# Moving the split weights to other byte offsets in SBUF: one layer of a hybrid decoder on one core

## The chip, the core and the metric

The kernel runs on one core of a Trainium2 chip. The metric is the device time of one execution, in microseconds (us). Before the change it is 1136.88 us, the median of three runs (1136.14, 1136.88 and 1137.68). The profile shown here is of one further execution, which took 1139.12 us.

## What is computed

One decoder layer over 512 tokens of width 1024, all in float32: a half-step SwiGLU feed-forward block (width 2816), a combined projection that feeds a gated spatial mixer and a dilated windowed attention, an output projection, cross-attention into 256 memory rows, a second half-step feed-forward block, and a last RMSNorm. In the reference's words:

```python
def swiglu(h, w_gate, w_up, w_down):
    return (jax.nn.silu(h @ w_gate) * (h @ w_up)) @ w_down

h = rmsnorm(x, ffn1_norm[l])
x = x + 0.5 * swiglu(h, ffn1_w_gate[l], ffn1_w_up[l], ffn1_w_down[l])
h = rmsnorm(x, mix_norm[l])
z = h @ w_in[l]
...
x = x + y @ w_out[l]
h = rmsnorm(x, cross_norm[l])
m = rmsnorm(mem, mem_norm[l])
x = x + memory_cross_attention(h, m, cross_wq[l], cross_wk[l], cross_wv[l], cross_wo[l])
h = rmsnorm(x, ffn2_norm[l])
x = x + 0.5 * swiglu(h, ffn2_w_gate[l], ffn2_w_up[l], ffn2_w_down[l])
return rmsnorm(x, final_norm)
```

## The kernel before

Activations are kept transposed: width on the 128 partitions, the 512 tokens along the free dimension, so the residual stream is eight tiles x0 to x7 of 128 x 512. To keep float32 accuracy at the rate of the rounded type float32r, every operand of a large product is split into a high part (rounded, made by an ACT copy) and a low part (the rest, made by a DVE subtraction): `hH, hL` for activations and `whi, wlo` for weights. A product is then three matmuls into one PSUM bank: high by high, high by low, low by high (`mm3`, L127 to L129).

Weights stream from HBM through `load_weight` (L109 to L119). It takes a raw tile `wraw`, sends the DMA for it on SP's queue, and splits it: ACT writes `whi` (L103), DVE writes `wlo` from `wraw` and `whi` (L104). Each of the three has three buffers of 4096 bytes per partition. In the feed-forward blocks, the query, key and output projections, the 128 x 128 block of `whi` or `wlo` is the stationary operand and the activations (512 tokens, or 256 memory rows) stream past it. In the two projections `z_block` (w_in) and the value projection of the cross-attention it is the other way round: a slice of the activations is stationary and 512 columns of `whi` or `wlo` stream. For most of the last down projection the split weights are kept: they are written into 2048-byte tiles of the activation pool instead (named `wk`), and they stream 256 tokens at a time, so that each half of the tokens can be finished apart.

The order of the work is the program's own order on each engine; the framework puts in the waits. `LAG`, `WARM` and `SB` are small numbers that set how far attention stages are skewed, how many matmuls on ones run at the start while the first weights arrive, and a buffer count.

What the change is about is where the tiles lie. Pools are laid one behind the other within each partition, in the order in which they are opened, and each tile takes a multiple of 32 bytes. The small pools end at byte 6944, which is 32 beyond a multiple of 128; a pool `fill` of `FILL = 56` words (224 bytes) follows, and so `base` (the residual stream) begins at 7168, a multiple of 1024. Every tile that a large matmul reads lies behind it, in pools whose tiles are multiples of 128 bytes: `hp` (40 tiles of 2048 bytes, the activations) begins at 37376, `wp` (three raw, three high and three low tiles of 4096 bytes) at 119296, 131584 and 143872, and the pool of the stage at hand (`ffn`, `mix` or `cross`) at 156160. All of these are multiples of 128, so before the change every operand of every large matmul begins at 0 beyond a multiple of 128.

```python
base = ctx.enter_context(tc.tile_pool(name="base", bufs=1))
hp = ctx.enter_context(tc.tile_pool(name="hp", bufs=40))
wp = ctx.enter_context(tc.tile_pool(name="wp", bufs=3))
```

Of the kernel before, what the change touches and what calls it, by code (L numbers as in the profile page):

```python
# [17 lines left out]
F32 = mybir.dt.float32  # L18
F32R = mybir.dt.float32r
# [5 lines left out]
P = 128  # L25
# [29 lines left out]
def body(tc, I, out):  # L55
    nc = tc.nc
    from contextlib import ExitStack
    ctx = ExitStack()
    with ctx:
# [3 lines left out]
        base = ctx.enter_context(tc.tile_pool(name="base", bufs=1))  # L63
        hp = ctx.enter_context(tc.tile_pool(name="hp", bufs=40))
        wp = ctx.enter_context(tc.tile_pool(name="wp", bufs=3))
        pacc = ctx.enter_context(tc.tile_pool(name="pacc", bufs=4, space=bass.MemoryType.PSUM))
        paux = ctx.enter_context(tc.tile_pool(name="paux", bufs=4, space=bass.MemoryType.PSUM))

# [33 lines left out]
        def split(hi, lo, src):  # L102
            ins = nc.scalar.activation(hi, src, AF.Copy)  # L103
            nc.vector.tensor_sub(lo, src, f32(hi))  # L104
            return ins
# [2 lines left out]

        def load_weight(src, shape, cuts=1):  # L109
            raw = wp.tile([P] + shape, F32, name="wraw", tag="wraw")  # L110
            hi = wp.tile([P] + shape, F32R, name="whi", tag="whi")
            lo = wp.tile([P] + shape, F32R, name="wlo", tag="wlo")
            step = shape[0] // cuts
            for c in range(cuts):
                p = slice(c * step, (c + 1) * step if c < cuts - 1 else shape[0])
                last["dma"] = nc.sync.dma_start(raw[:, p], src[:, p])
                last["hi"] = split(hi[:, p], lo[:, p], raw[:, p])
            return hi, lo
# [95 lines left out]
        def ffn(norm, gate, up, down, nxt, first=None, between=None):  # L214
            h = (norm.H, norm.L)
            with tc.tile_pool(name="ffn", bufs=2) as fp:
# [40 lines left out]
                for c in range(NCHUNK):  # L257
                    hid = ([], [])
                    for j in range(CF):
                        f = c * CF + j  # L260
                        ps = []
                        for src in (gate, up):
                            if f == 0 and src is gate and first is not None:
                                w = first()
                            else:
                                w = load_weight(src[f], [KD, P])
                            acc = acc_tile()
                            for k in range(KD):
                                mm3(acc, w, h, (slice(None), k), k, k == 0, k == KD - 1)
                            ps.append(acc)  # L270
                            if first is not None and f == 1 and R is None:
                                R = factor()
                        pending.append(ps)
                        if first is not None and f == 0:
                            continue
                        if R is None:
                            R = factor()
                        while pending:
                            evacuate(pending.pop(0), hid)
                    if c < NCHUNK - 1 or nxt is not None:  # L280
                        for d in range(KD):
                            w = [load_weight(down[c, d, :, j0:j1, :], [j1 - j0, P])
                                 for j0, j1 in halves]
                            down_tile(d, w, hid, slice(0, S), halves)
                            if c == NCHUNK - 1:
                                nxt.add(d)
                            elif between is not None:
                                between(d)
                        continue
# [5 lines left out]
                    def weights(d, keep):  # L295
                        if d in kept:
                            return kept[d], thirds
                        if not keep:
                            return [load_weight(down[c, d, :, j0:j1, :], [j1 - j0, P])
                                    for j0, j1 in halves], halves  # L300
                        kept[d] = []
                        for j0, j1 in thirds:
                            raw = wp.tile([P, j1 - j0, P], F32, name="wraw3", tag="wraw")
                            nc.sync.dma_start(raw, down[c, d, :, j0:j1, :])
                            pair = tuple(h_tile("wk")[:, :(j1 - j0) * P]
                                         .rearrange("p (j m) -> p j m", m=P) for _ in range(2))
                            split(*pair, raw)
                            kept[d].append(pair)
                        return kept[d], thirds
# [574 lines left out]
```

## Time and profile before

| what | before |
|---|---|
| median of three runs | 1136.88 us |
| the profiled execution | 1139.12 us |
| its span, first to last instruction | 1137.3 us |
| TensorE busy (PE) | 1121.1 us, 99% of the span, 5472 matmuls |
| weight loads (PEld) | 936.4 us, 82% |
| VectorE busy (DVE) | 589.2 us, 52% |
| ScalarE busy (ACT) | 422.6 us, 37% |
| GpSimd busy (POOL) | 66.2 us, 6% |
| mean granted TensorE clock | 0.993 |
| read from HBM | 107.78 MB, 97 GB/s over the span with the 2.10 MB written |

Rows of the profile name a group by the line in the kernel, the engine, the operation, and the tiles written and read (`acc<-hH,whi` is a matmul into `acc` whose moving operand is the first name and whose stationary operand is the second). PE is the row of the matmuls, PEld that of the weight loads. A matmul's time in a row runs from its start to the end that the profile models, so matmuls overlap each other in the records; how fast they follow one another is read from their start times.

### The profile page before, as it was taken

The numbers are of one execution on the slowest core, as the hardware profiler recorded it, in microseconds if no ns is written. First come the engines' busy times: TensorE is split into PE (matmuls) and PEld (weight loads), VectorE is DVE, ScalarE is ACT, GpSimd is POOL, SyncE is SP. The second block draws the span as 40 slices with busy tenths as digits, with TensorE's granted clock in tenths as the row PEclk, the third lists the DMA queues.
The fourth block names the chain that finished last, engine by engine and source line by source line (L and its number), as shares of the span: only waits on it lengthen the run. The fifth ranks groups of instructions, "written<-read, shape, count | busy, mean of one in ns | idle before, by whom it ended". The sixth has DMA issues, their size and how long they took to land. (4 is left out here: it accounts for less than half of the span.)

```text
span 1137.3 us, 13932 instructions
## 1 busy us (share of the span) xinstructions
PE 1121.1 (99%) x5472; PEld 936.4 (82%) x5472; DVE 589.2 (52%) x1023; ACT 422.6 (37%) x668; POOL 66.2 (6%) x82
## 2 busy tenths in 40 slices
PE   9999999999999999999999999999999999999996
PEld 7788888888888888877868988778888888888996
DVE  4544533444344456578797555455444334445542
ACT  6332322332233433567655344433222222233420
POOL 2000100000002000001121000120000000000011
PEclk9999999999999999999989999999999999999998
DMA  6322333222233423010135412132232333323511
GB/s 218 112 93 88 114 97 128 93 93 94 83 88 114 141 93 108 25 45 29 41 111 196 165 63 74 47 102 93 95 99 75 89 125 97 108 93 113 154 63 38
DMA packets 39698, 110.79 MB, mean 97 GB/s; under 512 B 4432, under 2 KB 9296, under 8 KB 39632
## 3 DMA queue, kind: packets, MB, share of 16 engines
q1 hardware_dynamic: 39632, 109.89, 30.1%
q8 instruction: 43, 0.70, 0.2%
q14 instruction: 23, 0.19, 0.1%
HBM read 107.78 MB, written 2.10 MB: 97 GB/s over the span
## 5 line engine op out<-in xcount | busy, mean ns | idle before, releaser
L103 ACT ACTIVATE whi<-wraw 128x1024 fp32r<-128x1024 f32 (+2 forms) x213 | 202.8, 953 | 522.0 <-PE acc L128 300.9
L104 DVE TENSOR_TENSOR wlo<-wraw,whi 128x1024 fp32r<-128x1024 f32 (+2 forms) x213 | 238.4, 1120 | 166.7 <-ACT whi L103 166.4
L127 PE MATMUL acc<-hH,whi 128*128 128x512 f32 x768 | 300.8, 392 | 0.6 <-ACT hH L202 0.6
L128 PE MATMUL acc<-hL,whi 128*128 128x512 f32 x768 | 299.3, 390 | 0.8 <-DVE hL L203 0.8
L129 PE MATMUL acc<-hH,wlo 128*128 128x512 f32 x768 | 299.3, 390 | 0.5 <-DVE wlo L104 0.5
L128 PEld LDWEIGHTS acc<-hL,whi 128*128 128x128 f32 x768 | 144.3, 188 | 31.6 <-DVE hL L203 1.5
L127 PEld LDWEIGHTS acc<-hH,whi 128*128 128x128 f32 x768 | 144.3, 188 | 31.6 <-ACT hH L202 1.0
L129 PEld LDWEIGHTS acc<-hH,wlo 128*128 128x128 f32 x768 | 144.2, 188 | 30.6 <-DVE wlo L104 1.0
L127 PE MATMUL acc<-hidH,whi 128*128 128x512 f32 (+1 forms) x308 | 115.5, 375 | 0.0
L129 PE MATMUL acc<-hidH,wlo 128*128 128x512 f32 (+1 forms) x308 | 115.3, 374 | 0.0
L128 PE MATMUL acc<-hidL,whi 128*128 128x512 f32 (+1 forms) x308 | 115.3, 374 | 0.0
L170 POOL TENSOR_TENSOR sq<-sq 128x512 f32<-128x512 f32 (+1 forms) x39 | 49.3, 1265 | 778.8 <-ACT sq L178 778.4
L247 DVE TENSOR_TENSOR u<-acc,R 128x512 f32<-128x512 f32 x44 | 30.4, 690 | 121.6 <-PE acc L129 121.6
L243 DVE TENSOR_TENSOR gp<-acc,R 128x512 f32<-128x512 f32 x44 | 30.4, 691 | 85.6 <-PE acc L129 81.7
L128 PEld LDWEIGHTS acc<-hidL,whi 128*128 128x128 f32 x308 | 58.0, 188 | 10.3
L127 PEld LDWEIGHTS acc<-hidH,whi 128*128 128x128 f32 x308 | 58.0, 188 | 10.2
L129 PEld LDWEIGHTS acc<-hidH,wlo 128*128 128x128 f32 x308 | 58.0, 188 | 10.2
L127 PE MATMUL acc<-whi,hH 128*128 128x512 f32 x160 | 62.6, 391 | 0.0
L129 PE MATMUL acc<-whi,hL 128*128 128x512 f32 x160 | 62.4, 390 | 0.0
L128 PE MATMUL acc<-wlo,hH 128*128 128x512 f32 x160 | 62.3, 389 | 0.0
L230 DVE SCALAR_TENSOR_TENSOR x<-acc,x 128x512 f32<-128x512 f32 (+1 forms) x40 | 23.3, 584 | 75.0 <-PE acc L129 75.0
L178 ACT ACTIVATE sq<-x 128x512 f32<-128x512 f32 (+1 forms) x48 | 26.0, 551 | 41.8 <-DVE x L230 39.2
(211 smaller groups left out, 1476.6 us busy)
## 6 DMA issues: line engine op xcount, KB each, us to landing
wraw<-up SPq DMA_DIRECT2D x44, 512.0 KB, 3.5
wraw<-gate SPq DMA_DIRECT2D x43, 512.0 KB, 3.4
wraw<-down SPq DMA_DIRECT2D x28, 384.0 KB, 3.1
wraw<-w_in SPq DMA_DIRECT2D x20, 512.0 KB, 3.5
wraw<-down SPq DMA_DIRECT2D x28, 320.0 KB, 2.8
wraw<-w_out SPq DMA_DIRECT2D x16, 256.0 KB, 2.6
wraw<-wv SPq DMA_DIRECT2D x8, 512.0 KB, 3.4
wraw<-wk SPq DMA_DIRECT2D x8, 512.0 KB, 4.0
```

The costliest lines, as they stand in the source:

```text
L103: ins = nc.scalar.activation(hi, src, AF.Copy)
L104: nc.vector.tensor_sub(lo, src, f32(hi))
L127: nc.tensor.matmul(ps, lhsT=aH, rhs=bH, start=start, stop=False)
L128: nc.tensor.matmul(ps, lhsT=aH, rhs=bL, start=False, stop=False)
L129: nc.tensor.matmul(ps, lhsT=aL, rhs=bH, start=False, stop=stop)
L170: nc.gpsimd.tensor_add(self.parts[0], self.parts[0], sq)
L178: nc.scalar.activation(sq, src, AF.Square)
L230: nc.vector.scalar_tensor_tensor(X[d][:, tok], acc, 0.5, X[d][:, tok], op0=ALU.mult, op1=ALU.add)
L243: nc.vector.tensor_mul(gp, ps[0], R)
L247: nc.vector.tensor_mul(u, ps[1], R)
```

## The change

`whi` and `wlo` leave `wp` and get pools of their own, `wh` and `wl`, each with three buffers as before. Three small pools with one tile each stand in between: 8 words (32 bytes) ahead of `wh`, 16 words (64 bytes) ahead of `wl`, and 104 words (416 bytes) behind it. Each pad tile is touched once by a memset of one element on DVE.

`wh` then begins at 131584 + 32 = 131616, which is 32 beyond a multiple of 128. Its three tiles are 12288 bytes, 96 times 128, and so `wl` begins at 131616 + 12288 + 64 = 143968, which is 96 beyond a multiple of 128. The last pad ends at 143968 + 12288 + 416 = 156672, a multiple of 512: the pool of the stage begins 512 bytes later than before, at 0 beyond a multiple of 128 again. The raw weights, the activations, the residual stream and the kept weights `wk` stay where they were or at that same residue. `load_weight` takes its two split tiles from the new pools; nothing else is edited.

```diff
@@ -63,6 +63,13 @@
         base = ctx.enter_context(tc.tile_pool(name="base", bufs=1))
         hp = ctx.enter_context(tc.tile_pool(name="hp", bufs=40))
         wp = ctx.enter_context(tc.tile_pool(name="wp", bufs=3))
+        wpad = ctx.enter_context(tc.tile_pool(name="wpad", bufs=1))
+        wh = ctx.enter_context(tc.tile_pool(name="wh", bufs=3))
+        wpad2 = ctx.enter_context(tc.tile_pool(name="wpad2", bufs=1))
+        wl = ctx.enter_context(tc.tile_pool(name="wl", bufs=3))
+        wpad3 = ctx.enter_context(tc.tile_pool(name="wpad3", bufs=1))
+        for pool, words, n in ((wpad, 8, "pad1"), (wpad2, 16, "pad2"), (wpad3, 104, "pad3")):
+            nc.vector.memset(pool.tile([P, words], F32, name=n)[:, 0:1], 0.0)
         pacc = ctx.enter_context(tc.tile_pool(name="pacc", bufs=4, space=bass.MemoryType.PSUM))
         paux = ctx.enter_context(tc.tile_pool(name="paux", bufs=4, space=bass.MemoryType.PSUM))
 
@@ -108,8 +115,8 @@
 
         def load_weight(src, shape, cuts=1):
             raw = wp.tile([P] + shape, F32, name="wraw", tag="wraw")
-            hi = wp.tile([P] + shape, F32R, name="whi", tag="whi")
-            lo = wp.tile([P] + shape, F32R, name="wlo", tag="wlo")
+            hi = wh.tile([P] + shape, F32R, name="whi", tag="whi")
+            lo = wl.tile([P] + shape, F32R, name="wlo", tag="wlo")
             step = shape[0] // cuts
             for c in range(cuts):
                 p = slice(c * step, (c + 1) * step if c < cuts - 1 else shape[0])
```

No instruction changes its place or its waits; the order differs only at the very start of DVE's program, by the three memsets. The first rows there before the change (the residual tile's number stands behind `x_`):

```order
L73 MEMSET pad 128x1
L78 MEMSET ones 128x128
L203 SCALAR_TENSOR_TENSOR hL<-x_84,gains,hH 128x512 [waits DMAHW1_49,DMAHW0_49,Activation_49]
L104 TENSOR_TENSOR wlo<-wraw,whi 128x512 [waits DMAHW2_49,Activation_49]
L104 TENSOR_TENSOR wlo<-wraw,whi 128x512 [waits DMAHW3_49,Activation_49]
```

and the same place after it, where line numbers are seven higher:

```order
L72 MEMSET pad_88 128x1
L72 MEMSET pad_90 128x1
L72 MEMSET pad_92 128x1
L80 MEMSET pad 128x1
L85 MEMSET ones 128x128
L210 SCALAR_TENSOR_TENSOR hL<-x_105,gains,hH 128x512 [waits DMAHW1_49,DMAHW0_49,Activation_49]
L111 TENSOR_TENSOR wlo<-wraw,whi 128x512 [waits DMAHW2_49,Activation_49]
L111 TENSOR_TENSOR wlo<-wraw,whi 128x512 [waits DMAHW3_49,Activation_49]
```

The memset of `ones`, for which the warm-up matmuls wait, now stands behind four small memsets instead of one.

## The prediction

> **What bounds the kernel now.** I read the page's busy times first. Its first part gives, for each engine, busy time, share of the span and number of instructions; the clock row gives the granted TensorE clock in 40 slices.
>
> ```profile
> PE 1121.1 (99%) x5472; PEld 936.4 (82%) x5472; DVE 589.2 (52%) x1023; ACT 422.6 (37%) x668; POOL 66.2 (6%) x82
> PEclk9999999999999999999989999999999999999998
> ```
>
> TensorE is busy 99% of the time, at full clock but for one slice and the end. Busy alone does not say whether it streams at its own pace or is kept waiting inside that 99%. So I looked next at stretches of the run (length in us, then busy time and count of each engine, granted clock, DMA share, GB/s).
>
> ```profile
> 60.00:150.00 90.00, 90.00 (x399) 74.57 (x398) 43.34 (x59) 28.25 (x39) 5.25 (x4) 1.00 0.32 101
> 450.00:600.00 150.00, 146.92 (x755) 115.50 (x754) 114.46 (x306) 90.69 (x203) 16.71 (x37) 0.98 0.17 54
> 780.00:1050.00 270.00, 270.00 (x1193) 223.71 (x1192) 120.49 (x147) 79.93 (x101) 0.00 (x0) 1.00 0.31 98
> ```
>
> In the feed-forward blocks PE has no idle time at all while DVE is busy 45% of the time (120.49 of 270): weights always arrive early. Only the attention stretch (450 to 600) has gaps, with DVE busy 114 of 150 us. So nearly all of the time is a number of matmuls multiplied by how fast they follow one another, and that is read from start times in the timeline. The first two rows are 18 matmuls apart with weights stationary, the next two 9 apart with weights moving, the last two 14 apart with 256 columns.
>
> ```profile
> 300.06 0.39 PE L127 MATMUL acc<-hH,whi 128*128 128x512 f32 x1
> ...
> 304.14 0.39 PE L127 MATMUL acc<-hH,whi 128*128 128x512 f32 x1
> ...
> 479.76 0.39 PE L127 MATMUL acc<-whi,hH 128*128 128x512 f32 x1
> ...
> 481.80 0.39 PE L127 MATMUL acc<-whi,hH 128*128 128x512 f32 x1
> ...
> 1069.73 0.28 PE L128 MATMUL acc<-hidL,wk 128*128 128x256 f32 x1
> ...
> 1071.41 0.28 PE L127 MATMUL acc<-hidH,wk 128*128 128x256 f32 x1
> ```
>
> 4.08 / 18 = 226.7 ns; 2.04 / 9 = 226.7 ns; 1.68 / 14 = 120.0 ns. The longer stretch agrees: 270 us with 1193 matmuls, two of them cut by its edges, is 270 / 1191 = 226.7 ns. Going from 256 to 512 columns costs 106.7 ns, so the columns of a 512-column matmul take 213.3 ns and **13.3 ns** are left that do not depend on the columns. These 13.3 ns are the only part of the steady pace that reading operands from another place could lower, and they are the same whichever operand moves and at all three places of the program. Blocks of a weight tile lie 512 bytes apart and activations 2048, so steps of 512 bytes between the two operands change nothing; steps of 32 occur in no large matmul before the change.
>
> **The change part by part.** It moves no instruction. It adds three memsets and moves two operands to starts that are 32 and 96 beyond a multiple of 128, both 32 beyond a multiple of 64. That it does so follows from the sizes in the diff, so a rival in which the tiles stay at 0 is out.
>
> *The matmuls on shifted weights.* They are counted from the groups by shape; the column behind the shape is the count, and each stands for three products.
>
> ```profile
> L127 PE MATMUL acc<-hH,whi 128*128 128x512 f32 x768 | 300.8, 392 | 0.6 <-ACT hH L202 0.6
> L127 PE MATMUL acc<-hidH,whi 128*128 128x512 f32 x264 | 103.1, 390 | 0.0
> L127 PE MATMUL acc<-whi,hH 128*128 128x512 f32 x160 | 62.6, 391 | 0.0
> L127 PE MATMUL acc<-hidH,wk 128*128 128x256 f32 x132 | 37.4, 284 | 0.0
> L127 PE MATMUL acc<-yH,whi 128*128 128x512 f32 x64 | 27.4, 431 | 0.6 <-DVE yo L619 0.6
> L127 PE MATMUL acc<-oH,whi 128*128 128x512 f32 x64 | 25.3, 395 | 0.0
> L127 PE MATMUL acc<-mH,whi 128*128 128x256 f32 x64 | 18.1, 283 | 0.0
> L127 PE MATMUL acc<-hidH,whi 128*128 128x256 f32 x44 | 12.5, 283 | 0.0
> L127 PE MATMUL acc<-whi,mH 128*128 128x512 f32 x32 | 12.5, 389 | 0.0
> ```
>
> Without `wk`, which stays at 0, these are 768 + 264 + 160 + 64 + 64 + 64 + 44 + 32 = 1460, times three 4380 matmuls. In 4380 - 576 = 3804 the weight is the stationary operand, in (160 + 32) x 3 = 576 it streams. What a start at 32 or 96 does to them no row shows, so it is bounded. Below: all 13.3 ns go, 4380 x 13.3 = 58.4 us less. Above: each takes one more piece of its operand; how that could count is worked out with the rivals, from 7 to 29 us. I take 0, because it is nearest to the rows: the pace is the same at every place and in every pairing of operands, and a stationary load has room.
>
> ```profile
> 300.07 0.19 PEld L128 LDWEIGHTS acc<-hL,whi 128*128 128x128 f32 x1
> 300.29 0.19 PEld L129 LDWEIGHTS acc<-hH,wlo 128*128 128x128 f32 x1
> ```
>
> A load starts with the matmul before the one that it serves and lasts 0.19 us in a spacing of 0.227: 37 ns are free. One piece more of eight would make it 24 ns longer (0.19 / 8) and still hide. If that cover were gone it would cost what rival B says.
>
> *The splits.* ACT writes `whi` at 32 and DVE reads it there and writes `wlo` at 96. The nearest rows are the two halves of the rotary step, the same DVE operation on 128 x 64 elements, in runs of eight words that begin at 0 in the first and 32 bytes later in the second (ns: least, median, most).
>
> ```profile
> L432 DVE TENSOR_TENSOR qk<-ra,rb x8: 218/224/228, 438.3 to 491.4; 128x64 f32<-128x64 f32 x8
> L433 DVE TENSOR_TENSOR qk<-ra,rb x8: 218/220/223, 438.5 to 491.6; 128x64 f32<-128x64 f32 x8
> ```
>
> Writing 32 bytes further on costs nothing there (220 against 224 ns). ACT has no such row. A split of 512 elements that took a piece more of 33 (64 bytes each) would last 20 ns longer on an engine. In the feed-forward blocks that is hidden, since PE has no idle time there. It counts where PE does wait for `wlo`, while the output projection's weights pass between 555 and 600 us (waits in us: total, times, longest; then the DMAs of these weights).
>
> ```profile
> PE acc L129 <- DVE wlo L104: 2.1, 1, 2.1
> ...
> wraw<-w_out SPq DMA_DIRECT2D x16, 256.0 KB, 2.6
> ```
>
> 16 weights by 20 ns on each of two engines are 0.6 us at most; I take 0.
>
> *The memsets.* Three on DVE ahead of `ones`, at the start:
>
> ```profile
> 0.81 0.06 DVE L73 MEMSET pad<- 128x1 f32 x1 [0.81 <-PEq L873]
> 0.86 0.17 DVE L78 MEMSET ones<- 128x128 f32 x1
> 7.12 0.63 ACT L103 ACTIVATE whi<-wraw 128x512 fp32r<-128x512 f32 x1 [1.94 <-DMA wraw<-gate]
> 8.55 0.50 PE L127 MATMUL acc<-hH,whi 128*128 128x512 f32 x1 [0.59 <-ACT hH L202]
> ```
>
> They are 3 x 0.06 = 0.18 us, and the warm-up matmuls start that much later. But at 8.55 us PE waits 0.59 us for an activation tile that ACT makes behind the second half of the first weight, and ACT waited for the DMA of that. The delay ends in that wait; were the cover gone it would be 0.18 us. I take 0.1.
>
> **The sum.** 0 for the matmuls, 0 for the splits, 0.1 for the memsets. The profiled execution took 1139.1 us, 1.8 us more than its span of 1137.3, and lies 2.2 us above the median of the runs; what is added to one is added to the other: 1136.9 + 0.1 = **1137.0 us**.
>
> **The rivals.** *A, faster.* The 13.3 ns are the price of two reads that meet: the stationary block is fetched while the moving operand streams, both from starts at 0, and apart they no longer collide. For it speaks that the 13.3 ns are constant and that the load runs wholly inside the stream before it (0.19 of 0.227 us). Against it: the two reads don't keep step. 128 columns load in 0.19 us while 512 stream in 0.213, so the stream runs past the load, and a shifted start moves the meeting without avoiding it. All of it would give 1136.9 - 58.4 = 1078.5 us, half of it 1107.7, a third 1117.4.
>
> The Trainium skill (TensorE: Matmul & The Clock Gate, "Wait — 56ns, not 53.3ns?") has 215.7 ns for 512 columns in bf16, 2.5 ns beyond the columns. If that were the floor here, A's full gain would be 4380 x 10.8 ns = 47 us and the time 1090 us, an estimate from that page. Against A, the page SBUF — State Buffer ("Who interferes with whom") gives PE two independent read ports, one for each operand. The trace shows the larger 13.3 ns but not where it comes from.
>
> *B, slower.* An operand that starts off a multiple of 64 takes a piece more: the 512 bytes of a stationary block are eight pieces of 64 from 0 and nine from 32 or 96. It decides if 64 bytes or more are fetched at once and if the 13.3 ns are what shows of the load. Then they grow by an eighth, 1.67 ns: 4380 x 1.67 = 7.3 us, 1144.2 us; by two eighths, 1151.5. If instead a piece holds up the stream by its 16 columns (106.7 / 256 x 16 = 6.7 ns), 29 us and 1166 us. For it: two unaligned starts and a cover that I only inferred. Against it: the room of 37 ns.
>
> By the Trainium skill (SBUF — State Buffer, "Specifications (TRN2)") lines are 16 bytes. 32 and 96 are multiples of that, so no operand would touch a line more and B would cost nothing; no row here tells the size of a fetch.
>
> *C, slower by little.* Only the streaming operand suffers, since its load has no cover: 576 x 6.7 ns = 3.9 us, 1140.8 us, all of it in `z_block` and the value projection.
>
> **How the numbers follow.** About 0.2% (2.3 us) is what a measurement of this kernel can tell from no change. The forecast gets 0.46: the steady pace has been equal wherever it was read. A gets 0.24, of which 0.13 for half of the overhead or more and 0.11 for a third or less. B gets 0.22, of which 0.07 for the 29 us and 0.15 for 7 to 15. C gets 0.08. So faster 0.24, same 0.46, slower 0.22 + 0.08 = 0.30. The range must leave out no more than the two far ends, 0.13 + 0.07 = 0.2: from A's third, 1118, to B's two eighths, 1152. The likeliest case's own range is 1136 to 1139.
>
> **What would show it.** Start times in the feed-forward blocks: 226.7 ns again for the forecast; between 213 and 226 for A; 228 or more for B. `wk`, at 120.0 ns, must not move in any case, and is the control within the run. For C only the stretch where weights stream slows, to some 233 ns. The splits must keep their means (the ns behind the comma):
>
> ```profile
> L103 ACT ACTIVATE whi<-wraw 128x1024 fp32r<-128x1024 f32 x139 | 147.2, 1060 | 376.9 <-PE acc L128 184.9 <-issue 150.2 <-PE acc L129 40.3
> L104 DVE TENSOR_TENSOR wlo<-wraw,whi 128x1024 fp32r<-128x1024 f32 x139 | 173.2, 1246 | 100.9 <-ACT whi L103 100.7
> ```
>
> For the memsets, the wait of 0.59 us at 8.55 must shrink by at most 0.18. The prediction is wrong if the spacing on shifted weights changes by more than half a nanosecond (4380 x 0.5 = 2.2 us), or if PE begins to wait for splits in the feed-forward blocks.

## The result: 1.7% slower, and the profile after

The changed kernel takes 1156.57 us (median of four runs, 1155.13 to 1156.86) against 1137.22 for the kernel before on the same chip: a ratio of 1.0169, with a 95% interval of 1.0151 to 1.0187. That is 19.3 us more (17.2 to 21.3), outside the forecast range and on the side of rivals B and C.

The busy times of the page after, in the same columns as before, and the granted clock:

```profile
PE 1138.4 (99%) x5472; PEld 934.1 (81%) x5472; DVE 589.8 (51%) x1026; ACT 422.9 (37%) x668; POOL 66.5 (6%) x82
PEclk9999999999999999999999999999999999999998
```

PE is as busy as it was, for 17 us longer and at full clock; the other engines do what they did. The stretches (length, then busy time and count of each engine, clock, DMA share, GB/s) show where the time went:

```profile
60.00:150.00 90.00, 90.00 (x389) 72.74 (x388) 42.06 (x58) 27.78 (x39) 5.27 (x4) 1.00 0.32 100
450.00:600.00 150.00, 147.25 (x764) 114.97 (x763) 108.53 (x300) 86.10 (x197) 13.33 (x35) 1.00 0.15 47
780.00:1050.00 270.00, 270.00 (x1164) 217.79 (x1164) 117.29 (x153) 76.71 (x94) 0.00 (x0) 1.00 0.29 94
```

In the same 270 us of feed-forward work PE gets through 1164 matmuls where it got through 1193, again without idle time. Two being cut by the edges, that is 270 / 1162 = 232.4 ns each, where it was 226.7. The start times agree. The first two rows are 18 matmuls apart with weights stationary, the next two are 6 apart with weights streaming, the next two 29 apart with 256 columns and shifted weights; the last two are kept weights `wk`, which were not shifted, 7 matmuls apart:

```profile
299.63 0.39 PE L134 MATMUL acc<-hH,whi 128*128 128x512 f32 x1
...
303.80 0.40 PE L134 MATMUL acc<-hH,whi 128*128 128x512 f32 x1
...
484.73 0.40 PE L134 MATMUL acc<-whi,hH 128*128 128x512 f32 x1
...
486.12 0.40 PE L134 MATMUL acc<-whi,hH 128*128 128x512 f32 x1
...
644.81 0.28 PE L134 MATMUL acc<-mH,whi 128*128 128x256 f32 x1
...
648.23 0.28 PE L136 MATMUL acc<-mH,wlo 128*128 128x256 f32 x1
...
1076.92 0.28 PE L134 MATMUL acc<-hidH,wk 128*128 128x256 f32 x1
...
1077.76 0.28 PE L135 MATMUL acc<-hidL,wk 128*128 128x256 f32 x1
```

4.17 / 18 = 231.7 ns, 1.39 / 6 = 231.7 ns, 3.42 / 29 = 117.9 ns, 0.84 / 7 = 120.0 ns. So 512-column matmuls on shifted weights became slower, 256-column ones became slightly *faster*, and the control did not move. Over all undisturbed steps of the two traces the means are 227.0 before and 232.2 after for weights that are stationary, 226.9 and 232.3 for weights that stream, 120.0 and 117.8 for 256 columns. That accounts for the loss: (4380 - 576 - 324) = 3480 stationary at 5.2 ns, 576 streaming at 5.4 ns, less 324 of 256 columns at 2.2 ns, is 18.1 + 3.1 - 0.7 = 20.5 us, inside the interval. (The two profiled spans differ by 16.0 us only: the profiled execution before lies 1.9 us above the median of its kernel, the one after 1.4 us below. A part of that may be the clock, which was 0.98 in the attention stretch before and 1.00 after; 2% of 150 us is 3 us, an estimate.)

The pace after is also no longer even. Where weights are stationary, the steps in the trace after run from 228 to 235 ns in an order that repeats, where before each step was 226 to 228 ns.

The splits kept their means (1060 and 1246 ns before):

```profile
L110 ACT ACTIVATE whi<-wraw 128x1024 fp32r<-128x1024 f32 x139 | 147.5, 1062 | 386.6 <-PE acc L135 189.0 <-issue 158.6 <-PE acc L136 36.3
L111 DVE TENSOR_TENSOR wlo<-wraw,whi 128x1024 fp32r<-128x1024 f32 x139 | 173.3, 1248 | 102.5 <-ACT whi L110 102.5
```

So the loss lies in TensorE's pace alone. The open questions were which property of the addresses sets it, and by what law.

### The profile page after: what moved, and what is told of

It is laid out like the page before. It is cut to its first block, busy times and chain, and to the rows that moved or that the text cites. A ratio compares the mean times of both kernels' runs of the same rounds, so it can differ in the third digit from the quotient of the medians.

```text
span 1153.3 us, 13935 instructions
## 1 busy us (share of the span) xinstructions
PE 1138.4 (99%) x5472; PEld 934.1 (81%) x5472; DVE 589.8 (51%) x1026; ACT 422.9 (37%) x668; POOL 66.5 (6%) x82
## 5 line engine op out<-in xcount | busy, mean ns | idle before, releaser
L134 PE MATMUL acc<-hH,whi 128*128 128x512 f32 x768 | 304.2, 396 | 0.0
L135 PE MATMUL acc<-hL,whi 128*128 128x512 f32 x768 | 303.1, 395 | 0.3 <-DVE hL L210 0.3
L136 PE MATMUL acc<-hH,wlo 128*128 128x512 f32 x768 | 302.9, 394 | 0.1
```

Source lines behind the costliest of these rows:

```text
L134: nc.tensor.matmul(ps, lhsT=aH, rhs=bH, start=start, stop=False)
L135: nc.tensor.matmul(ps, lhsT=aH, rhs=bL, start=False, stop=False)
L136: nc.tensor.matmul(ps, lhsT=aL, rhs=bH, start=False, stop=stop)
```

## The experiments

The theories are numbered as in the expectations. Theory 1 is rival B: a start off a multiple of 64 costs its own operand a piece more. Theory 2 is rival A's mechanism with either sign: what counts is how the starts of the two operands lie to one another. Theories 3 and 4 give theory 2 a period of 512 and of 256 bytes; theory 5 asks which pair it is.

### 1. The new pools with both weights at multiples of 128

```diff
-        for pool, words, n in ((wpad, 8, "pad1"), (wpad2, 16, "pad2"), (wpad3, 104, "pad3")):
+        for pool, words, n in ((wpad, 32, "pad1"), (wpad2, 32, "pad2"), (wpad3, 64, "pad3")):
```

> The changed kernel with its new pools, memsets and pads, but the pads sized so that the high and low weights both begin at 0 beyond a multiple of 128. Every theory that puts the loss on the byte offset expects the time of before, 1137 us, and 226.7 ns from one 512-column matmul to the next. If the loss came with the pools or memsets themselves, about 1156 us and 232 ns would stay.

Measured: 1158.58 us, a ratio of 1.0185 (1.0168 to 1.0202). This was meant as a control, and every theory that puts the loss on the offset expected 1137. The high weights now begin at 131712 and the low ones at 144128, multiples of 128 both, and the kernel is no faster than with the change. The stretch in the feed-forward block:

```profile
780.00:1050.00 270.00, 270.00 (x1160) 216.98 (x1159) 116.55 (x152) 76.01 (x93) 0.00 (x0) 1.00 0.29 93
```

270 / 1158 = 233.2 ns. Either the pools themselves cost this, or 128 is not the multiple that counts: modulo 512 the high weights lie at 128 and the low ones at 256, the activations at 0.

### 2. Everything shifted by 32 bytes together

```diff
-FILL = 56
+FILL = 64
```

> The kernel before with the fill of 56 words made 64, so that weights and activations, moving and stationary alike, all begin 32 beyond a multiple of 128. Theory 1 (a start off a multiple of 64 costs its operand a piece more, whatever the other operand does) expects the loss of the change or more, 1156 us or above, and the kept weights and the attention slowed too. Theory 2 (what counts is how the starts of the stationary and the moving operand lie to one another) expects 1137 us and 226.7 ns, since nothing is shifted against anything.

Measured: 1137.38 us, ratio 1.0000 (0.9991 to 1.0010).

```profile
780.00:1050.00 270.00, 270.00 (x1193) 223.65 (x1192) 120.86 (x147) 79.68 (x101) 0.00 (x0) 1.00 0.30 98
```

1193 matmuls, as before. No large operand lies at a multiple of 64 any more and nothing is lost: theory 1 and with it rivals B and C fall. What is left is how the operands lie to one another, or the new pools themselves, which this kernel does not have.

### 3. A table of residues, by TensorE alone

A kernel without the layer fills two stationary and two moving buffers and runs groups of 48 matmuls in the layer's order, each group with its own byte shifts of the four operands:

```python
for k in range(KD):
    for i, (l, r) in enumerate(((S_(st[0], sH, k), M_(mv[0], mH, k, n)),
                                (S_(st[0], sH, k), M_(mv[1], mL, k, n)),
                                (S_(st[1], sL, k), M_(mv[0], mH, k, n)))):
        nc.tensor.matmul(a[:, :n], lhsT=l, rhs=r, start=k == 0 and i == 0,
                         stop=k == KD - 1 and i == 2)
```

> No part of the layer: a table of spacings, the output is not the layer's. Groups of 48 float32r matmuls in the kernel's order (high weight by high activation, high by low, low by high, eight blocks, twice) with nothing to wait for, each group with its own byte residues of the stationary high and low part and of the moving high and low part; 512 columns, then nine groups of 256, then bf16 groups. Control (all at 0): 226.7 and 120.0 ns. The residues of the change (32, 96, 0, 0): 232 ns and 118 ns by either theory, if no other engine is needed for the effect; 226.7 if the splits on ACT and DVE are. Theory 1: every group with an operand at 32 or 96 is slow, also all at 32 or all at 96, and in proportion to the share of shifted reads. Theory 2: the groups with equal residues for both operands (all at 32, all at 64, all at 96) stay at 226.7, and moving the activations instead of the weights costs as much. A period of 64 bytes leaves weights at 64 at 226.7.

Measured, in ns from start to start over the last 24 matmuls of a group (shifts of stationary high, stationary low, moving high, moving low):

```
512 columns: 0,0,0,0     231.1     32,32,32,32  231.1
             32,96,0,0   233.3     64,64,64,64  231.1
             64,64,0,0   233.3     96,96,96,96  231.1
             0,0,32,32   231.1     4,4,4,4      237.8
             32,0,0,0    232.2     0,0,0,32     226.7
256 columns: 0,0,0,0     117.8     32,96,0,0    118.3
```

The control failed, for the reason that experiment 1 had just brought up: the buffers of this table begin at 384 (moving high), 0 (moving low), 128 and 256 (stationary) beyond multiples of 512. Read that way it says three things. No other engine is needed, since nothing else runs: the splits are out. A common shift by 32, 64 or 96 leaves the pace alone, as in experiment 2. And the slow pace is found with multiples of 128 as in experiment 1. The only group of 512 columns at 226.7 ns, (0, 0, 0, 32), shows that a single operand's shift can also take the 4.4 ns away; its four starts are not equal modulo 256.

The bf16 groups in the same run, one row for 47 recorded matmuls of the 48 with 512 columns and one for 48 with 256:

```profile
405.74 10.53 PE L148 MATMUL xf<-mvb,stb 128*128 128x512 bf16 x47
416.11 5.40 PE L148 MATMUL xg<-mvb,stb 128*128 128x256 bf16 x48
```

From the start of one group to that of the next are 10.37 us, 10.37 / 48 = 216.0 ns; and (5.40 - 0.27) / 47 = 109.1 ns for 256 columns. So beyond the 213.3 ns of the columns bf16 leaves some 2.5 ns and float32r 13.3 at its best. The former agrees with the 215.7 ns that the Trainium skill gives (TensorE: Matmul & The Clock Gate, "Wait — 56ns, not 53.3ns?"). The two bf16 buffers begin at 384 and 448 beyond multiples of 512, 64 bytes apart modulo 256, and nothing is lost there; no other placement was tried in bf16.

### 4. The same pools and pads, all pads ahead of the weights

```diff
         wpad = ctx.enter_context(tc.tile_pool(name="wpad", bufs=1))
-        wh = ctx.enter_context(tc.tile_pool(name="wh", bufs=3))
         wpad2 = ctx.enter_context(tc.tile_pool(name="wpad2", bufs=1))
-        wl = ctx.enter_context(tc.tile_pool(name="wl", bufs=3))
         wpad3 = ctx.enter_context(tc.tile_pool(name="wpad3", bufs=1))
+        wh = ctx.enter_context(tc.tile_pool(name="wh", bufs=3))
+        wl = ctx.enter_context(tc.tile_pool(name="wl", bufs=3))
```

> The changed kernel with the same pools, the same three pads and the same memsets, but with all pads ahead of both weight pools: 32 + 64 + 416 = 512 bytes, so that high and low weights and the pool of the stage begin 512 bytes later than before, at multiples of 512 like the activations. Theory 3 (what counts is the distance between the stationary and the moving start, taken modulo 512 bytes; 128 is not enough, as weights at multiples of 128 alone have shown) expects 1137 us and 226.7 ns. If pools, pads or memsets cost anything, or if the distance modulo more than 512 counts, more than 1140 us.

Measured: 1137.29 us, ratio 0.9999 (0.9990 to 1.0009), with 1193 matmuls in the stretch again:

```profile
780.00:1050.00 270.00, 270.00 (x1193) 223.65 (x1192) 121.29 (x148) 79.09 (x100) 0.00 (x0) 1.00 0.32 99
```

The control that experiment 1 should have been: three pads, two pools and three memsets cost nothing, and only where the weights lie matters.

### 5. The grid

The table again, with all buffers at multiples of 512, and the high and low stationary parts shifted by every multiple of 32 up to 480 against moving parts at 0, 24 matmuls a group.

> No part of the layer: a table of spacings, the output is not the layer's. All buffers begin at multiples of 512. 256 groups of 24 float32r matmuls of 512 columns in the kernel's order, with the high stationary part shifted by 0 to 480 bytes and the low one by 0 to 480, in steps of 32, against moving parts at 0; then equal shifts of 16, 48 and so on to 496; then equal shifts by 32 with 256 columns; then common shifts of both operands by 0, 4, 8, 16, 32 and 256 bytes. Theory 3: 226.7 ns at shift 0, 232 at (32, 96), 231 to 233 at (128, 256), values between 215.8 (the bf16 spacing of the first table, 213.3 for the columns and 2.5) and 238 elsewhere, and equal spacing for common shifts by 32 and 256. Theory 1 (each unaligned start costs its own operand a piece): at most three values, which depend on whether the shift is a multiple of 64. If some shift gives less than 226.7, the layer can gain from it: 4380 matmuls times the difference.

Measured, in ns from start to start over the last 12 of a group (rows: shift of the high part, columns: of the low part):

```
hi\lo        0     32     64     96    128    160    192    224
    0    226.7  233.3  230.3  233.1  231.2  233.3  231.1  231.2
   32    232.0  233.3  231.2  232.2  231.9  233.3  232.6  231.1
   64    233.3  235.5  233.3  231.2  231.1  232.2  232.1  231.8
   96    230.0  235.6  232.8  234.2  232.1  231.1  233.3  233.3
  128    233.3  231.1  230.0  233.3  232.8  233.3  233.8  232.2
  160    231.1  233.3  231.2  231.2  233.3  233.3  233.3  231.1
  192    228.8  228.8  233.3  228.9  231.1  233.3  228.9  231.1
  224    233.3  231.1  230.3  233.3  231.1  231.7  232.2  233.3
```

The cell of the change, (32, 96), has 232.2 ns; in the trace its group of 24 runs from the first row to the second, 23 steps of 231.7 ns:

```profile
127.52 0.39 PE L101 MATMUL gbd<-mvH,stH 128*128 128x512 f32 x1
...
132.85 0.40 PE L101 MATMUL gbd<-mvH,stL 128*128 128x512 f32 x1
```

The other three quarters, with one or both shifts 256 larger, repeat this within 0.3 ns in 62 of the 64 cells. One of the other two is (0, 0): its very first group, at the start of the program, still has steps of 427 ns until 25 us, and the 226.7 in the table is that of its three repeats. The other is (64, 32), with 235.5 ns where the low part lies at 32 and 231.1 where it lies at 288. **So the period is 256 bytes at 63 of 64 places, and 0 is the best of them all**: no multiple of 32 gives less than 226.7 ns. Equal shifts of 16, 48 and so on against moving parts at 0 gave 226.7 at 16 but 233.3 at 272, which is 16 again modulo 256, and 228.3 to 233.3 at the other odd multiples of 16, each the same 256 bytes further on. At (64, 32) and at 16 either the period is longer or what ran just before decides; the table can't tell which. With 256 columns the order turns round: 120.0 ns at 0 and at 160, 117.5 to 118.8 at all other shifts. Common shifts of both operands gave 226.7 for 32 and 256 bytes, but 237.8 for 4, 232.2 for 8 and 230.0 for 16: the common shifts below 32 bytes that were tried all cost something.

The grid also accounts for experiment 1, whose weights lie at (128, 0) modulo 256: 233.3 ns in the grid, and a mean of 233.3 ns for stationary weights in that trace.

### 6 and 7. What the grid foretells for the layer

Half of the change alone (low weights at 96, high ones at 0 modulo 256), and both weights at 192:

```diff
-        for pool, words, n in ((wpad, 8, "pad1"), (wpad2, 16, "pad2"), (wpad3, 104, "pad3")):
+        for pool, words, n in ((wpad, 64, "pad1"), (wpad2, 24, "pad2"), (wpad3, 40, "pad3")):
```

```diff
-        for pool, words, n in ((wpad, 8, "pad1"), (wpad2, 16, "pad2"), (wpad3, 104, "pad3")):
+        for pool, words, n in ((wpad, 48, "pad1"), (wpad2, 64, "pad2"), (wpad3, 16, "pad3")):
```

> Half of the change alone: the high weights at a multiple of 256 like the activations, only the low ones 96 bytes beyond. Theory 1 (a shifted operand pays for itself): a third of the products read low weights, so about a third of the loss of 19 us, 1143 to 1144 us. Theory 4 (the distance of stationary and moving start modulo 256 sets the pace of the whole sequence, as in the grid): the grid's (0, 96) has 233.1 ns against 226.7 for all three products, and where weights stream (0, 160) has 233.3; 3480 x 6.4 + 576 x 6.6 ns less 0.6 us for the 256-column matmuls is 25.5 us: 1160 to 1163 us, slower than the whole change although it shifts less.

> Both weight pools at 192 bytes beyond a multiple of 256, a multiple of 64. Theory 1: 192 is a multiple of 64, so no piece more: 1137 us. Theory 4: the grid's (192, 192) has 228.9 ns, and 64 (192 the other way round) 233.3 where weights stream: 3480 x 2.2 + 576 x 6.6 ns less 0.7 us is 10.8 us: 1146 to 1149 us.

Measured: the low weights alone 1157.08 us, ratio 1.0179 (1.0161 to 1.0197); both at 192 1146.48 us, ratio 1.0080 (1.0064 to 1.0096). The stretch in the first, then in the second:

```profile
780.00:1050.00 270.00, 270.00 (x1164) 217.57 (x1163) 116.58 (x152) 76.04 (x93) 0.00 (x0) 1.00 0.29 94
```

```profile
780.00:1050.00 270.00, 269.99 (x1179) 220.90 (x1178) 118.41 (x145) 78.10 (x96) 0.00 (x0) 1.00 0.30 96
```

232.4 and 229.4 ns. Both at 192 lands inside what the grid gave (1146 to 1149), where theory 1 had 1137; the layer's mean steps are 229.1 ns, and 233.3 where weights stream, against 228.9 and 233.3 in the grid. Shifting only the low weights costs as much as the whole change, not a third of it as theory 1 has it. It is 3 us less than the grid's 1160 to 1163: the layer's mean step is 232.5 ns where the grid has 233.1, and 231.2 where weights stream, against 233.3. For streaming weights the grid is only an analogy, since it shifts stationary parts alone. In these kernels its cells carry over to the layer to within about 2 ns.

The run with the low weights alone also shows that the whole sequence is slow, and not only the products that read a shifted block. Where weights are stationary, the two products that read unshifted operands alone are followed after 233.3 and 231.6 ns on average, the one that reads `wlo` after 232.7. The first of these steps, 233.3 ns, leads from one unshifted product to the other.

### 8. Both weights 256 bytes further on

```diff
         wpad = ctx.enter_context(tc.tile_pool(name="wpad", bufs=1))
-        wh = ctx.enter_context(tc.tile_pool(name="wh", bufs=3))
         wpad2 = ctx.enter_context(tc.tile_pool(name="wpad2", bufs=1))
+        wh = ctx.enter_context(tc.tile_pool(name="wh", bufs=3))
         wl = ctx.enter_context(tc.tile_pool(name="wl", bufs=3))
         wpad3 = ctx.enter_context(tc.tile_pool(name="wpad3", bufs=1))
-        for pool, words, n in ((wpad, 8, "pad1"), (wpad2, 16, "pad2"), (wpad3, 104, "pad3")):
+        for pool, words, n in ((wpad, 48, "pad1"), (wpad2, 16, "pad2"), (wpad3, 64, "pad3")):
```

> Both weight pools 256 bytes beyond a multiple of 512, everything else at a multiple of 512. Theory 4 with its period of 256 expects 1137 us and 226.7 ns; a period of 512 (theory 3) some 1155 us or more.

Measured: 1137.83 us, ratio 1.0005 (0.9996 to 1.0015), 1193 matmuls in the stretch:

```profile
780.00:1050.00 270.00, 270.00 (x1193) 223.58 (x1192) 121.29 (x148) 79.44 (x100) 0.00 (x0) 1.00 0.31 99
```

A shift by 256 costs nothing in the layer.

### 9. Are the 13.3 ns the load?

The table's sequence once more, with fewer stationary columns (`lhsT=l[:, :cols]`) and then with fewer moving ones.

> No part of the layer: a table of spacings, the output is not the layer's. The kernel's sequence with all operands at multiples of 512 and with the change's shift (32, 96): first with 128, 96, 64 and 32 stationary columns and 512 moving ones, then with 512, 448 and so on to 128 moving ones, then with one operand alone shifted by 4 or 8 bytes. If the 13.3 ns beyond the columns are the stationary load meeting the stream, they shrink with the stationary columns: 226.7, 224, 221 and 218.5 ns, down towards the 2.5 of bf16, and the change's extra 5.5 ns shrinks with them. If they are a fixed hand-over, 226.7 stays at every width. With fewer moving columns the extra of the shift should turn from a loss at 512 (232) to a gain at 256 (118 against 120).

Measured, in ns over the last 24 of each group:

```
stationary columns      128     96     64     32      (512 moving)
all at 0              226.7  230.0  230.0  231.7
shifted (32, 96)      232.2  232.2  230.0  228.9
moving columns          512    448    384    320    256    192    128   (128 stationary)
all at 0              226.7  206.7  173.3  146.7  120.0  111.7  111.7
shifted (32, 96)      232.2  203.3  173.3  147.2  118.1  111.7  111.7
```

Stationary parts alone at 4 or 8 bytes gave 232.5 and 230.8, moving parts alone 238.0 and 233.3. The loads did become shorter, with a median of 108 ns for 32 columns against 188 for 128. The load theory falls: with a quarter of the stationary columns the overhead does not shrink but grows, from 13.3 to 18.4 ns. The overhead beyond the columns (n / 2.4 ns) is 13.3 ns at 512, 384, 320 and 256 columns but 20 at 448, and the shift gains at 448 and 256, loses at 512 and does next to nothing at 384 and 320. A fixed price per load or per start does not give such a row. It looks like two trains of reads that settle into a common beat, and how good the beat is would depend on the length of both and on where they start; that is a guess, which no run here tests.

### 10. Which starts have to agree

One stationary and one moving buffer, with every second stationary and/or every second moving operand shifted by x:

```python
nc.tensor.matmul(a, lhsT=S_(st[0], so[i % 2], k), rhs=M_(mv[0], mo[i % 2], k, S),
                 start=i == 0, stop=i == 3 * KD - 1)
```

> No part of the layer: a table of spacings, the output is not the layer's. One stationary and one moving buffer, 512 columns, seven shifts x from 32 to 224 bytes, five sequences for each. own: every second matmul has both of its operands x further on. nxt: every second matmul has its moving operand x further on, and the stationary operand of the matmul behind it, which is loaded meanwhile, is x further on too. sta: only every second stationary operand is shifted. mov: only every second moving operand. all: every stationary operand. If what matters is the load against the stream under which it runs (theory 5), nxt stays at 226.7 ns for every x and own does not. If it is each matmul's own two operands, own stays at 226.7 and nxt does not. If both differ from 226.7, the step from one moving operand to the next counts too, and mov must be slow by itself.

Measured, in ns:

```
x           32     64     96    128    160    192    224      (0: 226.7)
own      233.6  231.7  234.3  228.3  233.7  231.7  233.3
nxt      232.5  231.7  230.0  230.0  230.0  233.3  230.0
sta      235.0  230.0  230.0  232.2  231.7  230.0  233.3
mov      231.7  230.8  230.0  230.0  235.0  226.7  230.0
all      233.3  233.3  234.4  232.1  233.3  228.9  233.3
```

Neither pairing stays at 226.7, so theory 5 and its rival both fall. Shifting nothing but every second moving operand is slow at six of seven places. The row `all`, with one moving buffer, repeats the diagonal of the grid within 0.7 ns. No single pair decides. With all starts of the sequence equal modulo 256 and at multiples of 32, the pace was 226.7 at every place tried; with unequal starts it was 226.7 at a few places only: `mov` at 192 here, (0, 0, 0, 32) in experiment 3, and the equal shift of 16 in experiment 5.

## Why the prediction was wrong

**What bounds the kernel** was right: the time is the number of matmuls times their spacing, and the loss of 19 us is 4056 spacings that grew by 5 ns, less the little that 324 of 256 columns gained. The wrong step is the one behind it: "I take 0, because it is nearest to the rows: the pace is the same at every place and in every pairing of operands". The pace was the same because every large operand of the kernel before began at a multiple of 512, twice the period of 256. The rows showed one and the same point of the law many times over; the text even said that steps of 32 occur nowhere, and then read the even pace as evidence about them. With no row off that point the honest reading was that the trace says nothing about the term. The term that was put at 0 measured 5.2 ns on 3480 stationary products and 5.4 on 576 streaming ones. The range failed with it: its upper end was B's two eighths, 3.3 ns for each product, and B's 6.7 ns, which are more than was measured, had been left out as a far end.

**The forecast took the 13.3 ns as a part that could only be lowered** and left their growth to rivals B and C. They grew to about 19.

**Rival B** had the right sign and a price range (7 to 29 us) that holds the 20.5 us, by the wrong mechanism. Experiment 2 puts all large operands off multiples of 64 and loses nothing; experiment 1 has all at multiples of 128 and loses everything; experiment 7 uses a multiple of 64 and loses 9 us. Nor did the room for a load decide: the shorter loads of experiment 9 leave more of it and the spacing grows. **Rival C** falls with it: streaming weights slowed by 5.4 ns, but stationary ones by 5.2, in a block of work six times as large.

**Rival A** was nearest in kind, two reads whose starts matter to one another, and had the wrong sign. Its counterargument, that the stream runs past the load so that a shift moves the meeting without avoiding it, failed: the pace differs from 226.7 in 63 of the grid's 64 cells. But A assumed that equal starts are where the reads collide. Equal starts are the best place in the grid for 512 columns, and for 256 they are among the worst (120.0 against 117.5 at the best).

Against A the prediction had set the statement of the Trainium skill (SBUF — State Buffer, "Who interferes with whom") that PE's two read ports are independent. For float32r the two reads are not independent in time: with TensorE alone at work, moving nothing but the stationary blocks takes the spacing from 226.7 to as much as 235.6 ns, and moving both by 32 bytes leaves it at 226.7. Whether that happens at the ports no run shows. Against B the prediction had set the lines of 16 bytes that the Trainium skill gives (SBUF — State Buffer, "Specifications (TRN2)"), since 32 and 96 are whole lines. Whole lines did not keep the pace: the change cost 19 us, and a common shift by 16 bytes costs 3.3 ns in the table. Here the measurement decides.

**The smaller terms were right.** The kept weights stayed at 120.0 ns, the splits at 1062 and 1248 ns, and pads, pools and memsets together cost nothing (experiment 4, ratio 0.9999). The sign that was named for the memsets can't be read: the warm-up matmuls began 0.09 us later (1.17 against 1.08 us), but their 40 took 7.28 us instead of 6.18 in this profile, and the wait of 0.59 us is not there at all. In the other profiles with the same memsets they took 6.10 to 7.68 us.

**What stays open.** The runs show that the starts of the operands relative to one another set the pace, and give its size for this sequence; they do not show what in TensorE makes it so. Why float32r keeps 13.3 ns beyond its columns where bf16 keeps 2.5, why a shorter load makes that worse, why 448 columns cost 6.7 ns more than the line through their neighbours, why the period is 256, and why two places of experiment 5 do not keep to it are not explained by any run here.

**Is there something to gain?** For 512 columns no place tried beats the kernel before. The 256-column matmuls, some 960 of them with those of attention, could gain 2 to 3 ns each by the measured spacings, an estimate of 2 to 3 us at the very most; but the weights of some and the activations of others share pools with 512-column work, which lost more. It was not tried, and no version here beats the kernel before.

## What to carry to other kernels

An even pace in a trace says nothing about a parameter that never varied in it: before forecasting "no effect", look whether any row lies off the present value, and if none does, measure it with a small table before touching the kernel. For dense float32r matmuls, keep the starts of all stationary and moving operands equal modulo 256 bytes, and at multiples of 32, when the streams are 512 wide; in this layer a few small pads between pools cost close to 2% without one large matmul edited. And measure spacing by start times or by counts in a fixed stretch: the busy share of PE read 99% in every version.

## What was not expected of the hardware

- The spacing of float32r matmuls depends on where all their operands start relative to each other, with a period of 256 bytes at 63 of 64 places: 226.7 to 235.6 ns for 512 columns in the grid.
- The sign depends on the width: at (32, 96) 5.5 ns are lost at 512 columns, 3.4 gained at 448, about 2 gained at 256, none either way at 384, 0.5 lost at 320.
- Starts 4, 8 or 16 bytes off a multiple of 512 cost even when both operands share them: 237.8 ns at 4 bytes, 232.2 at 8, 230.0 at 16.
- A stationary block of 32 columns is followed no faster than one of 128: 231.7 against 226.7 ns.
- With 192 moving columns and with 128 the spacing is the same, 111.7 ns, for 128 stationary columns.
